# An encoder layer on one Trainium2 core: S5 tables on VectorE alone, q, k, v ahead in priority, and u, q, k, v, z as products of fp32r halves

## The chip, the cores and the metric

The kernel runs on one core of a Trainium2 chip. The metric is the device time of one execution in microseconds. Three runs of the kernel before gave 893.8, 893.03 and 889.67 us, median 893.03. Engines are named as the profile names them: PE is TensorE, DVE VectorE, ACT ScalarE, POOL GpSimd, SP SyncE.

## What is computed

One encoder layer on a sequence of 512 tokens of width 1024, in fp32. After an RMS norm, one weight of 1024 x 2576 is multiplied in and its columns are split; the change touches the projections of u, q, k, v and z (512 columns each) and of 16 gate columns, and the tables of the S5 scan that consumes u.

```python
h = _rmsnorm(x, norm_mix)
u, q, k, v, z, beta_f, beta_b, a_f, a_b = _split_cols(h @ w_in[l])
# u: S5, a diagonal complex recurrence in both directions, 32 groups of 16 channels, 64 states
lam_bar = jnp.exp(lam * step)
b_bar = ((lam_bar - 1.0) / lam)[:, :, None] * b
bu = jnp.einsum('gpc,bsgc->bsgp', b_bar, u.astype(jnp.complex64))
...
# q, k, v: 5-tap depthwise conv, silu, l2 norm of q and k, then gated delta rule in chunks of 64,
# with a triangular solve for each chunk, head and direction; z gates the result by silu(z)
```

After the two mixers come an output projection, cross attention to a memory of 256 tokens, and a mixture of 32 experts, two for each token.

## The kernel before

Everything is transposed: the normed input lies as `ht`, 128 partitions x 8 x 512, and one projection of 128 output columns (`proj`) loads a weight tile `wst` of 128 x 8 x 128 by SP's queue and multiplies 8 pieces of it with 8 pieces of `ht` into one PSUM bank (`mm8`, L143). There are 20 of them: 4 for u, 12 for q, k and v, 4 for z. The memory's k and v projections use `mm8` as well, with `mt` in place of `ht`, 256 columns wide.

The order of the work is set in two ways. The program merges generators (`weave`), and within the order of the program a scheduler that simulates the timeline places each engine's instructions; each engine then runs its queue in order, and waits where an operand or a buffer isn't there. The stages, with the profile's times:

- 0 to 66 us: the norm's transposes (L125), the u projections, the gates (L539), and the S5 parameters, small operations on DVE, ACT and POOL. `pw` holds powers of the diagonal.
- 66 to about 214 us: `weave((qkv, 13), (s5, 9))`. One stream is the 12 projections of q, k, v; each result goes through ACT (`xp`, `cv`), four conv products on DVE (L639, `cv`), a silu, PE transposes (L648) and, for q and k, a norm (L661 to L674). The other stream is the S5 groups, 8 of them: for each group two complex tables of 128 x 2 x 512 are made by `cmul` (L225 to L230): `pm`, which PE transposes (L372) and ACT copies to `bct`, and `ca`, which SP stores to `ca_scr`. PE then multiplies `uperm` with `bct` (L404, into `U`) and `bb` with `ca` (L381), and DVE copies that into `wl` (L387 to L390). `pm`, `ca` and `bct` have one buffer each. Two tables by hand say which engine makes each: of the 16, 9 are made on POOL (`CA_ENG` and `PM_ENG`, 1 is POOL), 7 on DVE.
- about 202 to 300 us: `weave((inv, 16), (rest(), 13), (rec, 17))`. `gdn_inv` forms the triangular matrices in four blocks (PE L703, L716, L717; DVE `e` L707, `N` L720), transposes them (`NT`, L731 and L734), solves by substitution on DVE (L742, L744), transposes the result (`XT`, `XN`, L749 and L750) and multiplies halves on PE (L768 and after). `rest` is the four z projections and 8 steps of the memory's k and v projections; `rec` (L414 to L417) is the S5 recurrence, 62 steps of four small DVE operations on `U`.
- about 300 to 435 us: `gdn_chain` beside the rest of the memory's projections and of `rec`, then the S5 output. 435 to 600 us: output projection and cross attention, whose products are already formed of fp32r halves by `mm3` (L149 to L151): each operand is split in a high part rounded to fp32r and a low part, the remainder, and low x high, high x high and high x low are added up. From 600 us: the experts.

Of the kernel before, what the change touches and what calls it, by code (L numbers as in the profile page):

```python
# [9 lines left out]
F32 = mybir.dt.float32  # L10
F32R = mybir.dt.float32r
# [20 lines left out]
P = 128  # L32
# [11 lines left out]
def weave(*streams):  # L44

    live = [[g, n, 0] for g, n in streams]
    while live:
        s = min(live, key=lambda t: (t[2] + 0.5) / t[1])
        s[2] += 1
        if next(s[0], s) is s:  # L50
            live.remove(s)


CA_ENG = (1, 1, 0, 1, 1, 1, 0, 1)
PM_ENG = (0, 0, 1, 0, 1, 0, 1, 0)


class Enc:
# [44 lines left out]
        return t  # L103


    def rms_T(self, pool, tiles, gain, out, tag, between=None, junk=None):

        nc = self.nc
        n = len(tiles)
        ss = pool.tile([P, 8], F32, name=tag + "ss", bufs=1)  # L110
        rs = pool.tile([P, 8], F32, name=tag + "rs", bufs=1)
        xn = []
        for i, t in enumerate(tiles):
            sq = junk if junk is not None else pool.tile([P, D], BF16, name=tag + "sq", bufs=1)
            nc.scalar.activation(sq, t, AF.Square, accum_out=ss[:, i:i + 1])
            nc.vector.tensor_scalar(ss[:, i:i + 1], ss[:, i:i + 1], 1.0 / D, 1e-6, op0=OP.mult, op1=OP.add)
            nc.gpsimd.tensor_tensor(rs[:, i:i + 1], ss[:, i:i + 1], self.nhalf[:, 0:1], op=OP.pow)
            nc.vector.tensor_scalar(t, t, rs[:, i:i + 1], None, op0=OP.mult)
            xn.append(t)
        if between:  # L120
            between()
        for k in range(8):
            ps = self.ps("tp")
            for i in range(n):
                nc.tensor.transpose(ps[:, i * P:(i + 1) * P],  # L125
                                    xn[i].rearrange("t (p k) -> t k p", k=8)[:, k, :], self.ident)
            src = ps[:, :n * P]
            if k % 2:
                nc.vector.tensor_scalar(out[:, k, :], src, gain[:, k:k + 1], None, op0=OP.mult)
            else:  # L130
                nc.scalar.activation(out[:, k, :], src, AF.Copy, scale=gain[:, k:k + 1])
        return xn

    def wcols(self, src, w):

        t = self.wp.tile([P, 8, w], F32, name="wst", bufs=4)
        self.nc.sync.dma_start(t, src)
        return t

    def mm8(self, ps, w, act):  # L140

# [12 lines left out]
    def stage_a(self):  # L154
        nc, tc, A = self.nc, self.tc, self.A
        pool = self.pa
        gain = self.col8('norm_mix', self.cp)
        x2d = A['x'][0]
        xt = []
        with tc.tile_pool(name="xp", bufs=1) as xp:  # L160
            for i in range(4):
                t = xp.tile([P, D], F32, name=f"x{i}")
                nc.sync.dma_start(t, x2d[i * P:(i + 1) * P, :])
                xt.append(t)
            self.ht = pool.tile([P, 8, T], F32, name="ht")
            self.pre = {}

            def first_weights():
                for c0 in (0, P):
                    self.pre[c0] = self.wcols(self.w_in(c0, P), P)  # L170
                self.w_g = self.wp.tile([P, 8, 16], F32, name="wg", bufs=1)
                nc.sync.dma_start(self.w_g, self.w_in(2560, 16))

            self.rms_T(xp, xt, gain, self.ht, "h", first_weights)

    def w_in(self, c0, w):
        return self.A['w_in'][0].rearrange("(p k) n -> p k n", k=8)[:, :, c0:c0 + w]

    def proj(self, c0):

        w = self.pre.pop(c0, None)
        if w is None:
            w = self.wcols(self.w_in(c0, P), P)
        ps = self.ps("mm")
        self.mm8(ps, w, self.ht)
        return ps

    def proj_u(self):
# [32 lines left out]
    def cmul(self, eng, pool, ore, oim, are, aim, bre, bim, shape, tag):  # L221
# [7 lines left out]
        eng.tensor_tensor(oim, aim, bre, op=OP.mult)  # L229
        eng.tensor_tensor(oim, oim, t2, op=OP.add)  # L230

    def s5_params(self):
        nc, A, tc = self.nc, self.A, self.tc
        sp = self.s5p
        v, g_ = nc.vector, nc.gpsimd
        with tc.tile_pool(name="s5t", bufs=1, side="right") as tq:
            ct = tq.tile([P, 2, 32, 16], F32, name="ct")
            dT = tq.tile([16, 32], F32, name="dT")
            aF = tq.tile([P, 2, 8, 32], F32, name="aF")
            aR = tq.tile([P, 2, 8, 32], F32, name="aR")  # L240
            bb = tq.tile([P, 2, 34, 16], F32, name="bb")
            b1 = tq.tile([P, 2, 32, 16], F32, name="b1")
            with tc.tile_pool(name="s5i", bufs=1, side="right") as tp:
                lamrow = tp.tile([32, 2, 128], F32, name="lamrow")
                for di, dn in enumerate('fb'):
# [26 lines left out]
                for ri in range(2):  # L272
                    ps = self.ps("s5")
                    for b in range(4):
                        nc.tensor.transpose(ps[:, b * P:(b + 1) * P], crow[:, ri, b, :], self.ident)
                    nc.scalar.activation(ct[:, ri].rearrange("p g c -> p (g c)"), ps, AF.Copy, scale=1.0 - 2.0 * ri)
# [66 lines left out]
                self.cmul(v, tp, b1[:, 0], b1[:, 1], bg(pw[:, 0, 1]), bg(pw[:, 1, 1]), bb[:, 0, :32], bb[:, 1, :32], [32, 16], "d")  # L343
            yield
            with tc.tile_pool(name="s5l", bufs=1, side="right") as tl:

# [5 lines left out]
                for gg in range(8):  # L352
# [3 lines left out]
                    bm = lambda b, ri: b[:, ri, gs, None, :].to_broadcast([P] + shp)  # L356

                    pm = tl.tile([P, 2] + shp, F32, name="pm", bufs=1)
                    e = PM_ENG[gg]
                    self.cmul((v, g_)[e], tl, pm[:, 0], pm[:, 1], am(aF, 0), am(aF, 1), bm(b1, 0), bm(b1, 1), shp, f"P{1 - e}")  # L360

                    ca = tl.tile([P, 2] + shp, F32, name="ca", bufs=1)
                    e = CA_ENG[gg]
                    self.cmul((v, g_)[e], tl, ca[:, 0], ca[:, 1], am(aR, 0), am(aR, 1),
                              bm(ct, 0), bm(ct, 1), shp, f"P{1 - e}")
                    nc.sync.dma_start(self.ca_scr[gg], ca.rearrange("p r g m c -> p (r g m c)"))

                    bcT = tl.tile([P, 4, 2, P], F32, name="bct", bufs=1)
# [148 lines left out]
    def gates(self):  # L517
# [6 lines left out]
        with tc.tile_pool(name="gt_", bufs=1) as tp:  # L524
# [9 lines left out]
            sel = tp.tile([P, 16], F32, name="gsel")  # L534
            v.tensor_reduce(sel, self.ident.rearrange("p (i c) -> p c i", i=4)[:, :16], axis=AX.X, op=OP.add)
            for j in range(2):
                for i in range(4):
                    k = j * 4 + i
                    nc.tensor.matmul(ps[i * 32:i * 32 + 16], self.w_g[:, k], self.ht[:, k], start=(j == 0), stop=(j == 1))  # L539
            for i in range(4):  # L540
                nc.scalar.activation(gT[i * 32:i * 32 + 16], ps[i * 32:i * 32 + 16], AF.Copy)
            pt = self.ps("tp")
# [133 lines left out]
    def proj_z(self):  # L676
        nc = self.nc
        for h in range(4):
            ps = self.proj(2048 + h * P)
            z = self.wp.tile([P, T], F32, name="zt", tag="ut", bufs=1)  # L680
            nc.scalar.activation(z, ps, AF.Silu)
            nc.sync.dma_start(self.z_scr[:, h], z)
            yield
# [823 lines left out]
    def build(self):  # L1507
# [41 lines left out]
        with tc.tile_pool(name="gi", bufs=2) as gi:  # L1549
            qkv = self.gdn_in([(w, n, h) for h in range(4) for w, n in ((1, "k"), (0, "q"))] +  # L1550
                              [(2, "v", h) for h in range(4)], gi)
            s5 = self.s5_params()
            next(s5)
            for _ in u:
                pass
            weave((qkv, 13), (s5, 9))

        self.gp2 = pool(left, "gp2")
        self.gp3 = pool(left, "gp3")
# [218 lines left out]
```

## Time and profile before

| what | value |
|---|---|
| median of 3 runs | 893.03 us |
| the profiled execution | 892.26 us |
| its span in the profile | 890.5 us |
| mean granted clock of PE | 0.948 |
| PE busy | 783.1 us (88%) |
| DVE, ACT, POOL busy | 404.3, 329.4, 232.6 us |
| projections from `ht` (L143) on PE | 151.3 us in 320 instructions |
| memory read, written | 165.50, 26.18 MB |

The profiled execution is 1.8 us longer than its span, and 0.8 us shorter than the median. A busy PE is not PE at its peak: matmuls are pipelined and the records of neighbours overlap, so the distance from start to start tells more than a record's length. PE's fp32 matmuls are two instructions each, which is why 160 matmuls of the projections are 320. Idle time is shown with what ended it, as the name of an engine and the tile that it wrote. Where a group's mean mixes cases (an operation that runs alone, or beside another engine), the timeline separates them.

### The profile page before, as it was taken

What the parts mean: (1) busy time and instruction counts of PE and PEld (TensorE: products, weight loads), DVE (VectorE), ACT (ScalarE), POOL (GpSimd) and SP (SyncE); (2) the same over time, 40 slices, a digit from 0 to 9 for tenths busy, and PEclk for the clock granted to TensorE, in tenths of its full rate; (3) what the DMA queues carried; (4) which work ended last, traced back from release to release, by engine and by line L of the source; (5) the groups of instructions that cost most, each with busy time, mean ns of one, the idle gap of its engine ahead of it and who ended that gap; (6) DMA issues with size and microseconds to landing.
All of it is one profiled execution on the core that took longest, in us unless ns stands there. A gap on an engine that the chain in (4) does not pass through costs nothing. (4 is left out here: it accounts for less than half of the span.)

```text
span 890.5 us, 12981 instructions
## 1 busy us (share of the span) xinstructions
PE 783.1 (88%) x4735; PEld 492.2 (55%) x4736; DVE 404.3 (45%) x1044; ACT 329.4 (37%) x760; POOL 232.6 (26%) x237
## 2 busy tenths in 40 slices
PE   5986998998997997899899999996698878788983
PEld 3443554555586875676688879895333333333331
DVE  4288767678899522244643554324210000000375
ACT  4242454455413235465343464333232131312204
POOL 1022857832100111205161332241311011100103
PEclk9996998999997998999999999998799999999997
DMA  7837222322663308615663714595699999999982
GB/s 206 144 91 111 74 78 74 100 76 98 225 193 104 108 24 169 116 56 172 184 224 96 260 49 159 194 406 187 248 391 412 414 411 408 395 391 410 410 350 102
DMA packets 128130, 185.17 MB, mean 208 GB/s; under 512 B 38734, under 2 KB 93006, under 8 KB 123968
## 3 DMA queue, kind: packets, MB, share of 16 engines
q1 hardware_dynamic: 122736, 172.31, 57.6%
q0 software_dynamic: 5328, 12.01, 3.6%
q8 instruction: 38, 0.62, 0.3%
q14 instruction: 28, 0.23, 0.1%
HBM read 165.50 MB, written 26.18 MB: 215 GB/s over the span
## 5 line engine op out<-in xcount | busy, mean ns | idle before, releaser
L143 PE MATMUL bank<-ht,wst 128*128 128x512 f32 x320 | 151.3, 621 | 4.2 <-ACT kd L583 2.4
L1340 PE MATMUL bank<-mw,xt 128*64 128x512 f32 x360 | 104.5, 595 | 1.5 <-DMA mw<-in_moe_w_up_dram 1.5
L143 PEld LDWEIGHTS bank<-ht,wst 128*128 128x128 f32 x320 | 60.7, 198 | 73.4 <-issue 68.3
L1344 DVE SCALAR_TENSOR_TENSOR hs<-hs,tw,bank 128x256 f32<-128x256 f32 x16 | 7.7, 480 | 168.9 <-ACT hs L1343 168.9
L1343 ACT ACTIVATE hs<-bank,tw 128x256 f32<-128x256 f32 x16 | 7.6, 474 | 155.5 <-PE bank L1340 155.5
L1380 PE MATMUL bank<-mw,hT 128*64 128x512 f32 x152 | 50.6, 660 | 16.2 <-ACT yd L1385 16.2
L1340 PEld LDWEIGHTS bank<-mw,xt 128*64 128x64 f32 x360 | 33.5, 138 | 55.6 <-issue 52.4
L143 PE MATMUL bank<-mt,wst 128*128 128x256 f32 x256 | 59.9, 393 | 0.0
L639 DVE SCALAR_TENSOR_TENSOR cv<-xp,taps,cv 128x512 f32<-128x512 f32 x48 | 50.4, 1049 | 20.8 <-ACT cv L637 19.7
L972 POOL TENSOR_TENSOR wlo<-wst,whi 128x1024 fp32r<-128x1024 f32 x16 | 38.6, 2416 | 78.7 <-ACT whi L971 78.7
L143 PEld LDWEIGHTS bank<-mt,wst 128*128 128x128 f32 x256 | 50.0, 198 | 7.7 <-issue 0.6
L1320 POOL DMA_INDIRECT xg<-t_scr,tidx x16 | 16.5, 1029 | 136.4 <-PE bank L1327 133.4
L824 POOL TENSOR_TENSOR kt<-kn,kd 64x512 f32<-64x512 f32 x14 | 14.5, 1035 | 97.6 <-PE bank L778 49.8
L1330 ACT ACTIVATE xt<-bank,gm 128x128 f32<-128x128 f32 x128 | 34.7, 382 | 8.9 <-PE bank L1327 7.8
L149 PE MATMUL bank<-wlo,oh 128*128 128x256 f32 x128 | 36.6, 289 | 0.0
L854 DVE SCALAR_TENSOR_TENSOR S<-S,egl,bank 128x128 f32<-128x128 f32 x48 | 15.5, 345 | 46.1 <-PE bank L851 46.1
L150 PE MATMUL bank<-whi,oh 128*128 128x256 f32 x128 | 35.8, 283 | 0.0
L1380 PEld LDWEIGHTS bank<-mw,hT 128*64 128x64 f32 x152 | 14.0, 148 | 38.7 <-issue 20.8
L151 PE MATMUL bank<-whi,ol 128*128 128x256 f32 x128 | 35.3, 287 | 0.0
L149 PE MATMUL bank<-mlo,mxh 128*128 128x512 f32 x64 | 25.8, 405 | 0.8 <-DVE gss L484 0.8
L903 POOL TENSOR_TENSOR mlo<-mst,mhi 128x512 fp32r<-128x512 f32 x16 | 22.0, 1393 | 14.8 <-ACT mhi L902 14.2
L150 PE MATMUL bank<-mhi,mxh 128*128 128x512 f32 x64 | 25.7, 402 | 0.0
(551 smaller groups left out, 1826.3 us busy)
## 6 DMA issues: line engine op xcount, KB each, us to landing
mw<-in_moe_w_down_dram SPq DMA_DIRECT2D x23, 1024.0 KB, 14.7
mw<-in_moe_w_gate_dram SPq DMA_DIRECT2D x45, 512.0 KB, 8.3
mw<-in_moe_w_up_dram SPq DMA_DIRECT2D x45, 512.0 KB, 13.9
wst<-in_w_in_dram SPq DMA_DIRECT2D x20, 512.0 KB, 4.5
ca_scr<-ca SPq DMA_DIRECT2D x8, 512.0 KB, 2.7
wst<-in_xa_wk_dram SPq DMA_DIRECT2D x8, 512.0 KB, 4.3
y_scr<-lhc SPq DMA_DIRECT2D x2, 2048.0 KB
wst<-in_xa_wv_dram SPq DMA_DIRECT2D x8, 512.0 KB, 4.3
```

What stands on the lines that cost most here:

```text
L143: self.nc.tensor.matmul(ps, w[:, k, :], act[:, k, :], start=(k == 0), stop=(k == 7))
L149: self.nc.tensor.matmul(ps, ah, bl, start=(first and i == 0), stop=False)
L150: self.nc.tensor.matmul(ps, ah, bh, start=False, stop=False)
L151: self.nc.tensor.matmul(ps, al, bh, start=False, stop=(last and i == n - 1))
L639: v.scalar_tensor_tensor(cv, xp[:, w:w + T], taps[:, w, m:m + 1], cv, op0=OP.mult, op1=OP.add)
L854: v.scalar_tensor_tensor(sn, S[di, h], self.egl[:, ch % 2, ch // 2, di * 4 + h:di * 4 + h + 1], p, op0=OP.mult, op1=OP.add)
L903: nc.gpsimd.tensor_tensor(lo[:, k], st, hi[:, k].bitcast(F32), op=OP.subtract)
L972: nc.gpsimd.tensor_tensor(lo, st, hi.bitcast(F32), op=OP.subtract)
L1320: self.gather = g_.indirect_dma_start(out=xg, out_offset=None, in_=self.t_scr, in_offset=bass.IndirectOffsetOnAxis(ap=self.tidx[:, q:q + 1 ...
L1330: nc.scalar.activation(xt[:, k], ps[:, (k % 4) * P:(k % 4 + 1) * P], AF.Copy, scale=self.gm[:, k:k + 1])
L1340: nc.tensor.matmul(pg[w * 64:w * 64 + 64].rearrange("p (a n) -> p a n", a=2), xt[:, k, w * 64:w * 64 + 64], un[k // 4 * 2 + w][:, :, k % 4 ...
L1380: nc.tensor.matmul(py[w * 64:w * 64 + 64], hT[:, k, w * 64:w * 64 + 64], wd[w][:, k, c], start=(k == 0), stop=(k == 1))
```

## The change

Three things are changed.

- The 16 S5 tables are all made on DVE, by `cprod`: four products of 128x512 and one addition of 128x1024, in place of four products and two additions of 128x512. For that `ct` and `b1` get a third, negated row, so that the subtraction becomes an addition; two copies on ACT fill these rows.
- The generator of q, k and v is stepped under `tc.high_priority()` (`ahead`), so that the scheduler prefers its instructions.
- `proj` uses `mm3`: `rms_T` writes the normed input as two fp32r tiles, `hth` (ACT) and `htl` (DVE, the remainder), and `wsplit` forms `whi` (ACT) and `wlo` (a subtraction) of every weight tile. `wlo` is formed on DVE for u2, u3 and all of q, k, v, and on POOL for u0, u1 and z. `wst` has 3 buffers in place of 4, `whi` and `wlo` two each. A projection is 24 matmuls. The gate columns are multiplied in fp32 with both halves, 16 matmuls in place of 8.

```diff
+def ahead(tc, g):
+    while True:
+        with tc.high_priority():
+            if next(g, g) is g:
+                return
+        yield
...
             src = ps[:, :n * P]
-            if k % 2:
+            if lo is not None:
+                nc.scalar.activation(out[:, k, :], src, AF.Copy, scale=gain[:, k:k + 1])
+                nc.vector.scalar_tensor_tensor(lo[:, k, :], src, gain[:, k:k + 1], out[:, k, :].bitcast(F32),
+                                               op0=OP.mult, op1=OP.subtract)
+            elif k % 2:
...
-        t = self.wp.tile([P, 8, w], F32, name="wst", bufs=4)
+        t = self.wp.tile([P, 8, w], F32, name="wst", bufs=3)
...
+    def wsplit(self, src, w, lo_eng):
+        st = self.wcols(src, w)
+        hi = self.wp.tile([P, 8, w], F32R, name="whi", bufs=2)
+        lo = self.wp.tile([P, 8, w], F32R, name="wlo", bufs=2)
+        self.nc.scalar.activation(hi, st, AF.Copy)
+        lo_eng.tensor_tensor(lo, st, hi.bitcast(F32), op=OP.subtract)
+        return hi, lo
...
-    def proj(self, c0):
-        w = self.pre.pop(c0, None)
-        if w is None:
-            w = self.wcols(self.w_in(c0, P), P)
+    def proj(self, c0, lo_eng=None):
+        hi, lo = self.pre.pop(c0, None) or self.wsplit(self.w_in(c0, P), P, lo_eng or self.nc.vector)
         ps = self.ps("mm")
-        self.mm8(ps, w, self.ht)
+        self.mm3(ps, [((hi[:, k, :], lo[:, k, :]), (self.hth[:, k, :], self.htl[:, k, :])) for k in range(8)])
         return ps
...
+    def cprod(self, pool, o, am, a, bm, b):
+        v = self.nc.vector
+        t = pool.tile(list(o.shape), F32, name="cpt", bufs=1)
+        for ri in range(2):
+            v.tensor_tensor(o[:, ri], am(a, 0), bm(b, 1 + ri), op=OP.mult)
+            v.tensor_tensor(t[:, ri], am(a, 1), bm(b, ri), op=OP.mult)
+        v.tensor_tensor(o, o, t, op=OP.add)
...
-                    e = PM_ENG[gg]
-                    self.cmul((v, g_)[e], tl, pm[:, 0], pm[:, 1], am(aF, 0), am(aF, 1), bm(b1, 0), bm(b1, 1), shp, f"P{1 - e}")
+                    self.cprod(tl, pm, am, aF, bm, b1)
...
-                    e = CA_ENG[gg]
-                    self.cmul((v, g_)[e], tl, ca[:, 0], ca[:, 1], am(aR, 0), am(aR, 1),
-                              bm(ct, 0), bm(ct, 1), shp, f"P{1 - e}")
+                    self.cprod(tl, ca, am, aR, bm, ct)
...
-                for i in range(4):
-                    k = j * 4 + i
-                    nc.tensor.matmul(ps[i * 32:i * 32 + 16], self.w_g[:, k], self.ht[:, k], start=(j == 0), stop=(j == 1))
+                for part in (self.htl, self.hth):
+                    for i in range(4):
+                        k = j * 4 + i
+                        nc.tensor.matmul(ps[i * 32:i * 32 + 16], self.w_g[:, k], part[:, k].bitcast(F32),
+                                         start=(j == 0 and part is self.htl), stop=(j == 1 and part is self.hth))
...
-            ps = self.proj(2048 + h * P)
+            ps = self.proj(2048 + h * P, nc.gpsimd)
...
-            weave((qkv, 13), (s5, 9))
+            weave((ahead(tc, qkv), 13), (s5, 9))
```

The change adds 29 lines ahead of the S5 stage, so a line there has a number higher by 27 to 29 in the kernel changed; the new products are L256 to L258, `wlo` is L157, and `mm3` L169 to L171.

The change also moves work. On DVE, at the first tables, the queue before reads as follows (`P` are the temporaries of `cmul`, `b_392` is `b1`, `cv` the conv products, `mt` the memory's norm, `dd` a small diagonal).

```order
L348 MEMSET dd 128x128
L225 TENSOR_TENSOR P_637<-aF,b_392 128x512
L226 TENSOR_TENSOR P_638<-aF,b_392 128x512
L593 COPY csr<-sbe 64x4x4 x2
L227 TENSOR_TENSOR pm<-aF,b_392 128x512
L229 TENSOR_TENSOR pm<-aF,b_392 128x512
L350 TENSOR_TENSOR dd<-ident,dT 16x128 x4
L228 TENSOR_TENSOR pm<-pm,P_637 128x512
L230 TENSOR_TENSOR pm<-pm,P_638 128x512
L225 TENSOR_TENSOR P_754<-aF,b_392 128x512
L226 TENSOR_TENSOR P_755<-aF,b_392 128x512
L639 SCALAR_TENSOR_TENSOR cv<-xp,taps,cv 128x512 x2
```

And the same place of DVE's queue in the kernel changed (`cpt` is the temporary of `cprod`).

```order
L157 TENSOR_TENSOR wlo<-wst,whi 128x1024
L668 SCALAR_TENSOR_TENSOR cv<-xp,taps,cv 128x512
L378 MEMSET dd 128x128
L256 TENSOR_TENSOR pm<-aF,b_449 128x512 x2
L257 TENSOR_TENSOR cpt<-aF,b_449 128x512
L256 TENSOR_TENSOR ca<-aR,ct 128x512 x2
L257 TENSOR_TENSOR cpt<-aF,b_449 128x512
L668 SCALAR_TENSOR_TENSOR cv<-xp,taps,cv 128x512
L380 TENSOR_TENSOR dd<-ident,dT 16x128 x4
L140 TENSOR_SCALAR mt<-bank_418,c_norm_mem 128x256
L157 TENSOR_TENSOR wlo<-wst,whi 128x1024
L258 TENSOR_TENSOR pm<-pm,cpt 128x1024
```

Now the table `ca` of the first group stands on DVE too, and the subtractions for `wlo` stand between the tables' operations.

On PE, at the start of the inverse, the queue before has a z projection (the L143 rows with `bank_1801` and `bank_1868`; `bank_1688` is a v projection) between one block and the next (a block is L703, then L716 and L717).

```order
L143 MATMUL bank_1688<-ht,wst 128x512 x4
L648 MATMUL bank_1708<-ident,cv 128x128 x4
L703 MATMUL bank_1750<-lef,g 64x64 x8
L703 MATMUL bank_1750<-geb,g 64x64 x8
...
L143 MATMUL bank_1801<-ht,wst 128x512 x8
L703 MATMUL bank_1817<-lef,g 64x64 x8
L703 MATMUL bank_1817<-geb,g 64x64 x7
L648 MATMUL bank_1719<-ident,cv 128x128 x4
...
L143 MATMUL bank_1868<-ht,wst 128x512 x8
L703 MATMUL bank_1884<-lef,g 64x64 x8
```

In the kernel changed the same place reads as follows; `bank_2199` and `bank_2286` are z1 and z2, L431 and L408 are the matmuls of the last S5 group, and L732, L745 and L746 those of the blocks.

```order
L171 MATMUL bank_2199<-hth,wlo 128x512
L169 MATMUL bank_2286<-htl,whi 128x512
L170 MATMUL bank_2286<-hth,whi 128x512
L431 MATMUL bank_1928<-uperm,bct 64x64 x2
...
L677 MATMUL bank_2026<-ident,cv 128x128 x4
...
L732 MATMUL bank_2057<-lef,g 64x64 x8
L732 MATMUL bank_2057<-geb,g 64x64 x8
L745 MATMUL bank_2165<-kT 64x64
L746 MATMUL bank_2165<-qT,kT 64x64
...
L732 MATMUL bank_2144<-lef,g 64x64 x8
```

z0, z1 and two matmuls of z2 have moved ahead of the last S5 group and so of the blocks, and blocks 0 and 1 now follow each other without a projection between them. Ten of the memory's projections, in place of nine, stand ahead of the matmuls on `XT` and `N` (L768 before, L797 now).

## Rows read from the trace of the kernel before

**Rows 1.** The page's slices, 40 of 22.3 us: PE's busy tenths.
```profile
PE   5986998998997997899899999996698878788983
```
**Rows 2.** The windows: us, then each engine's busy time, PE's clock, DMA share, GB/s.
```profile
66.00:202.00 136.00, 122.88 (x827) 65.59 (x826) 99.52 (x141) 60.12 (x168) 78.38 (x82) 0.92 0.35 85
202.00:281.00 79.00, 70.74 (x480) 49.60 (x479) 72.96 (x297) 25.14 (x36) 10.38 (x6) 0.97 0.54 174
281.00:435.00 154.00, 142.09 (x1186) 109.21 (x1183) 66.66 (x186) 73.02 (x155) 31.88 (x47) 0.93 0.44 110
600.00:890.00 290.00, 231.92 (x1141) 100.64 (x1139) 64.47 (x151) 74.75 (x218) 49.27 (x57) 0.93 0.89 349
```
**Rows 3.** Groups by line, 66 to 202 us, PE: busy, mean ns, idle before and releaser.
```profile
L143 PE MATMUL bank<-ht,wst 128*128 128x512 f32 x170 | 83.0, 635 | 0.0
L381 PE MATMUL bank<-ca,bb 64*32 64x128 f32 x256 | 13.7, 286 | 4.0 <-POOL xp L634 4.0
L404 PE MATMUL bank<-uperm,bct 128*64 128x64 f32 x256 | 11.3, 228 | 1.4 <-ACT bct L373 1.4
L372 PE MATMUL bank<-ident,pm 128*128 128x128 f32 x64 | 10.2, 292 | 7.6 <-DVE pm L228 7.4 <-POOL pm L230 0.2
```
**Rows 4.** The same groups, 66 to 202 us, DVE.
```profile
L639 DVE SCALAR_TENSOR_TENSOR cv<-xp,taps,cv 128x512 f32<-128x512 f32 x44 | 47.4, 1077 | 20.8 <-ACT cv L637 19.7
```
**Rows 5.** The timeline of DVE: start, us, instruction, idle before.
```profile
66.24 0.69 DVE L225 TENSOR_TENSOR P<-aF,b 128x512 f32<-128x512 f32 x1
66.85 0.68 DVE L226 TENSOR_TENSOR P<-aF,b 128x512 f32<-128x512 f32 x1
...
97.73 5.07 DVE L639 SCALAR_TENSOR_TENSOR cv<-xp,taps,cv 128x512 f32<-128x512 f32 x4 [4.22 <-ACT cv L637]
...
104.41 1.75 DVE L229 TENSOR_TENSOR ca<-aR,ct 128x512 f32<-128x512 f32 x1
...
113.93 3.11 DVE L639 SCALAR_TENSOR_TENSOR cv<-xp,taps,cv 128x512 f32<-128x512 f32 x4 [3.38 <-ACT cv L637]
```
**Rows 6.** The timeline of POOL at the same place.
```profile
102.22 1.72 POOL L228 TENSOR_TENSOR pm<-pm,P 128x512 f32<-128x512 f32 x1
```
**Rows 7.** The timeline of PE: gates, a projection, a block and the z behind it.
```profile
27.67 1.91 PE L539 MATMUL bank<-ht,wg 128*16 128x512 f32 x16
...
35.18 7.03 PE L143 MATMUL bank<-ht,wst 128*128 128x512 f32 x16
...
225.47 0.69 PE L703 MATMUL bank<-lef,g 128*64 128x64 f32 x16
...
227.53 7.13 PE L143 MATMUL bank<-ht,wst 128*128 128x512 f32 x16
```
**Rows 8.** The timeline of PE in the mix stage, products of halves.
```profile
457.47 0.40 PE L149 MATMUL bank<-mlo,mxh 128*128 128x512 f32 x1
457.70 0.39 PE L150 MATMUL bank<-mhi,mxh 128*128 128x512 f32 x1
```
**Rows 9.** Groups by line, whole span: splitting weights and halves, an add of 128x1024.
```profile
L972 POOL TENSOR_TENSOR wlo<-wst,whi 128x1024 fp32r<-128x1024 f32 x16 | 38.6, 2416 | 78.7 <-ACT whi L971 78.7
L971 ACT ACTIVATE whi<-wst 128x1024 fp32r<-128x1024 f32 x16 | 17.0, 1062 | 17.5 <-PE bank L151 10.7 <-DMA wst<-in_xa_wq_dram 4.6 <-issue 1.6
L1733 DVE TENSOR_TENSOR xr<-xr,yb 128x1024 f32<-128x1024 f32 x8 | 9.5, 1217 | 1.7 <-DMA yb<-y_scr 1.7
L1002 DVE TENSOR_TENSOR kvl<-kvs,kvh 128x1024 fp32r<-128x1024 f32 x4 | 6.2, 1562 | 10.0 <-ACT kvh L1001 10.0
```
**Rows 10.** Groups by line, 202 to 281 us, PE and DVE.
```profile
L143 PE MATMUL bank<-mt,wst 128*128 128x256 f32 x144 | 31.2, 379 | 0.0
...
L417 DVE TENSOR_TENSOR U<-U,rt 128x64 f32<-128x64 f32 x44 | 9.5, 216 | 0.5
L720 DVE SCALAR_TENSOR_TENSOR N<-bank,beta,e 128x64 f32<-128x64 f32 x32 | 6.7, 276 | 4.1 <-ACT e L710 4.1
```
**Rows 11.** The timeline of PE at the first matmuls behind the solve.
```profile
280.68 6.82 PE L768 MATMUL bank<-XT,N 32*32 32x32 f32 x128 [5.81 <-issue]
```

More of the change, by code (lines that the diff above doesn't have):

```diff
@@ L51, in weave @@
             live.remove(s)
-CA_ENG = (1, 1, 0, 1, 1, 1, 0, 1)
-PM_ENG = (0, 0, 1, 0, 1, 0, 1, 0)
+def ahead(tc, g):
[4 more added lines that the diff above has]
+        yield
 class Enc:
@@ L103, in colt, with rms_T @@
         return t
-    def rms_T(self, pool, tiles, gain, out, tag, between=None, junk=None):
+    def rms_T(self, pool, tiles, gain, out, tag, between=None, junk=None, lo=None):
         nc = self.nc
@@ L164, in stage_a @@
                 xt.append(t)
-            self.ht = pool.tile([P, 8, T], F32, name="ht")
+            self.hth = pool.tile([P, 8, T], F32R, name="hth")
+            self.htl = pool.tile([P, 8, T], F32R, name="htl")
             self.pre = {}
@@ L169, in first_weights @@
                 for c0 in (0, P):
-                    self.pre[c0] = self.wcols(self.w_in(c0, P), P)
+                    self.pre[c0] = self.wsplit(self.w_in(c0, P), P, nc.gpsimd)
                 self.w_g = self.wp.tile([P, 8, 16], F32, name="wg", bufs=1)
                 nc.sync.dma_start(self.w_g, self.w_in(2560, 16))
-            self.rms_T(xp, xt, gain, self.ht, "h", first_weights)
+            self.rms_T(xp, xt, gain, self.hth, "h", first_weights, lo=self.htl)
     def w_in(self, c0, w):
         return self.A['w_in'][0].rearrange("(p k) n -> p k n", k=8)[:, :, c0:c0 + w]
-    def proj(self, c0):
-        w = self.pre.pop(c0, None)
-        if w is None:
-            w = self.wcols(self.w_in(c0, P), P)
+    def proj(self, c0, lo_eng=None):
+        hi, lo = self.pre.pop(c0, None) or self.wsplit(self.w_in(c0, P), P, lo_eng or self.nc.vector)
         ps = self.ps("mm")
-        self.mm8(ps, w, self.ht)
+        self.mm3(ps, [((hi[:, k, :], lo[:, k, :]), (self.hth[:, k, :], self.htl[:, k, :])) for k in range(8)])
         return ps
@@ L236, in s5_params @@
         with tc.tile_pool(name="s5t", bufs=1, side="right") as tq:
-            ct = tq.tile([P, 2, 32, 16], F32, name="ct")
+            ct = tq.tile([P, 3, 32, 16], F32, name="ct")
             dT = tq.tile([16, 32], F32, name="dT")
@@ L241, in s5_params @@
             bb = tq.tile([P, 2, 34, 16], F32, name="bb")
-            b1 = tq.tile([P, 2, 32, 16], F32, name="b1")
+            b1 = tq.tile([P, 3, 32, 16], F32, name="b1")
             with tc.tile_pool(name="s5i", bufs=1, side="right") as tp:
@@ L275, in s5_params @@
                         nc.tensor.transpose(ps[:, b * P:(b + 1) * P], crow[:, ri, b, :], self.ident)
-                    nc.scalar.activation(ct[:, ri].rearrange("p g c -> p (g c)"), ps, AF.Copy, scale=1.0 - 2.0 * ri)
+                    nc.scalar.activation(ct[:, 1 + ri].rearrange("p g c -> p (g c)"), ps, AF.Copy, scale=1.0 - 2.0 * ri)
+                nc.scalar.activation(ct[:, 0].rearrange("p g c -> p (g c)"), ps, AF.Copy)
                 tl = lambda s: tp.tile([P, 32], F32, name="q" + s)
@@ L342, in s5_params @@
                 self.cmul(v, tp, bb[:, 0, :32], bb[:, 1, :32], bg(fre), bg(fim), bt[:, 0], bt[:, 1], [32, 16], "d")
-                self.cmul(v, tp, b1[:, 0], b1[:, 1], bg(pw[:, 0, 1]), bg(pw[:, 1, 1]), bb[:, 0, :32], bb[:, 1, :32], [32, 16], "d")
+                self.cmul(v, tp, b1[:, 1], b1[:, 2], bg(pw[:, 0, 1]), bg(pw[:, 1, 1]), bb[:, 0, :32], bb[:, 1, :32], [32, 16], "d")
+                nc.scalar.activation(b1[:, 0], b1[:, 2], AF.Copy, scale=-1.0)
             yield
```

## The prediction

> **What bounds the kernel now.** I read the page's slices first. PE is at 8 or 9 tenths over most of the span [rows 1], so the whole-kernel busy shares say little, and I went on by stage. The windows give three facts. From 66 to 202 us, the stretch in which q, k and v are projected beside the S5 tables, PE is busy 122.9 of 136 us while VectorE shows 99.5 and GpSimd 78.4 [rows 2]. From 202 to 281 us VectorE is the fuller engine, 73.0 of 79 us, with PE at 70.7 [rows 2]. From 600 us on DMA is at 0.89 [rows 2]: the expert weights bound that part, and their loads start when the stages ahead hand back SBUF, so whatever is gained ahead should move this tail as a whole.
>
> Next I asked what PE does in the first stretch. 83.0 us of its busy time are fp32 projections; the S5 matmuls and table transposes are 13.7, 11.3 and 10.2 us [rows 3]. The idle rows show that the tables can hold PE: 7.4 us are put down to VectorE's pm, and 4.0 us to GpSimd's xp, a small memset that stands behind table work on GpSimd [rows 3].
>
> Then I asked why VectorE is so busy. Its conv products cost 1.08 us each on average [rows 4]. Four of them in a row take 3.11 us from 113.93, while GpSimd is quiet, but 5.07 from 97.73 [rows 5], when GpSimd runs a pm table, 1.72 us for one of its subtractions [rows 6]. The tables' own 128x512 products start 0.61 us apart when GpSimd is quiet, and one takes 1.75 beside it [rows 5]. So two engines that both read large tiles slow one another. VectorE's idle time there is mostly for ScalarE's cv, 19.7 us in all [rows 4]: for the next projection to arrive.
>
> **The change, part by part.** All terms are against the profiled execution, 892.26 us (span 890.5); the median of the runs is 0.8 us above it.
>
> *Projections.* Before, a projection is 16 PE instructions and lasts 7.03 to 7.13 us [rows 7]. After it is 24 fp32r matmuls; in the mix stage such matmuls start 0.23 us apart [rows 8]: 24 x 0.23 = 5.5 us, so 1.5 us less, twenty times. The four u projections give back 6 us; against it stand the gate matmul, which doubles, +1.9 us [rows 7], the splitting of their own weights, two of them on GpSimd, and PE's wait for both halves of the norm's output. I count the u part as zero, between 4 us lost and 5 gained.
>
> *Splitting the weights.* Each wst now needs a rounded copy on ScalarE, 1.06 us, and a remainder [rows 9]. ScalarE has room. On VectorE no 128x1024 subtraction of this form exists; the plain add of that shape takes 1.22 and the nearest fp32r remainder 1.56 [rows 9]; I take 1.2, since it has the same two SBUF operands as the add. Nine such remainders lie among the tables (the others before the first table or on GpSimd), 10.8 us, at most 14. On GpSimd each takes 2.4 us [rows 9]; four are z's, late, when no table is left there.
>
> *Tables.* Sixteen tables, each four 128x512 products and one 128x1024 add: 4 x 0.61 + 1.22 = 3.7 us, 58 in all. Seven were on VectorE already and cost the same there alone (6 x 0.61); nine come over from GpSimd, +33 us. In return VectorE's slowed operations go back to their lone price: 44 conv products from 1.08 to 0.78 (a quarter of the 3.11), some 13 us, and its two ca tables up to 12 x (1.75 - 0.61) = 14.
>
> The sum for VectorE, from the first table to the first step of the recurrence: tables 58, conv 34, remainders 11, all else (wl, dd, vc, ss, mt) about 11: 114 us. For PE in the same stretch, 12.5 projections at 5.55 are 69, and its other work is the window's busy time less the projections, 122.9 - 83.0 = 40, taken as 46 since records of both overlap: 115 us. So the two are level. PE's idle time was 13 us there; I keep a little over half, 8, since GpSimd's part of it goes but single buffers (ca, pm) and two of whi and wlo stay. The first table starts at 66.2 now [rows 5]; two remainders, 2.4 us, come ahead of it, so 69. The recurrence then starts at 69 + 115 + 8 = 192 us, in place of 201.7.
>
> *Order around the inverse.* Before, z projections stand between the inverse's blocks, 7.13 us each [rows 7], and VectorE's block work waits on them. After, two z and the first matmuls of a third are ahead of block 0, and no conv product follows the first recurrence step. From that step to the XT,N matmuls, which now start at 280.7 [rows 11], 79 us pass. After, PE has 1.9 z (10.5 us), four blocks of 2.1 (225.47 to 227.53, [rows 7]) and ten kv projections in place of nine, 31.2 / 9 = 3.47 each [rows 10]: 54 us. VectorE had 73.0 us; by the order, 115 recurrence instructions stand ahead of XT in place of 176, each 0.22 us [rows 10], so 13 less, and conv, 3 less: 57, and 4 for ScalarE's e, as now [rows 10]: 61. VectorE sets it: XT,N at 192 + 61 = 253, that is 27.7 us earlier, plus 3.5 for the kv projection that no longer follows: 31 us. The 61 recurrence instructions that now come behind XT lie in VectorE's slack, busy 66.7 of 154 us there [rows 2].
>
> 892.3 - 31 = 861, and I forecast **861 us**. SP carries ca_scr stores and wst loads in one queue; a wst load that waits for VectorE's remainder holds back the ca store behind it, and so the next ca: 2.7 us eight times if never covered, covered here by the next pm (3.7 us).
>
> [...]
>
> **Rivals.**
> - *VectorE doesn't get faster.* If the slowed operations have another cause than GpSimd, VectorE's load is 99.5 + 33 + 11 = 143 us in the stretch, the recurrence starts at 69 + 143 = 212, XT,N at 273: 7.7 + 3.5 earlier, **881**. Against it: the same instruction has both durations, by whether GpSimd runs. 0.10.
> - *The engines trip over each other.* PE's projection needs ScalarE's rounding, which needs a free buffer from the projection two earlier, and VectorE's remainder in a queue of tables. With two full engines in order, the idle time of before (13 on PE) stays and 10 more come: the recurrence at 207, XT,N at 268, **876**. For it: the 7.4 us for pm [rows 3]. 0.16.
> - *Slower: the remainder becomes the wait.* If for each projection PE waits through one table (3.7) and the rounding (1.06) before the remainder is there, 12.5 x 4.7 = 58 us come on top of 115: the recurrence at 242, XT,N at 303, 22 later, with the kv projection's 3.5 back **911**. It decides against the change from about 2.5 us of wait per projection (31 us of gain over 12.5). For it: in-order VectorE, two buffers. Against it: PE has 46 us of other work to put between. 0.06; milder forms that end level, 0.08.
> - *Projections no faster.* If fp32r with alternating weights ran at the 0.40 us that a record lasts instead of the 0.23 us spacing [rows 8], 24 would last 9.4 us, +2.3 each, slower by some 25. The spacing in the mix stage has the same three-product pattern, so 0.02, within the slower chance.
>
> **How the numbers follow.** The main case, 0.58, has its own range from 847 (no stall left and a first table at 64) to 874 (lone prices high: remainder 1.56, stalls 20). With the first two rivals the time is under 888.5 in 0.84. What a measurement can tell from no change is about 0.5%, 4.5 us. Level 0.08, slower 0.08. The range of 8 in 10 runs from 844 to 885.
>
> **What would show it.** Right: four conv products in 3.1 us throughout; GpSimd near empty from 70 to 170 us; 24 matmuls in 5.5 us; the first recurrence step near 192 and XT,N near 253. Wrong: PE idle after 70 us put down to wlo or ca; remainders of 2 us; an unchanged 79 us from recurrence to XT,N; a clock below 0.9 where PE now waits; or a shift at XT,N that the tail from 600 us does not show.

## The result, and the profile after

The changed kernel takes 878.41 us, median of four executions (872.87 to 885.89), against 891.75 for the kernel before beside them (889.67 to 893.8): a ratio of 0.9856, interval 0.9815 to 0.9896. It is faster by 1.4%, less than half as much as forecast: 861 us would have been a ratio of 0.965. The profiled execution took 872.87 us, with a span of 871.1 and a mean granted clock of 0.932, where before it was 890.5 and 0.948. It is the fastest of the four; the slowest, 885.89 us, ran at a mean clock of 0.915, so the readings below account for 19.4 us of gain, and the median keeps 13.3 of them. Of the ten executions each of the kernels tables and mt_w8 below, the two slowest, over 1.5% above their fastest and at a lower clock, are left out of medians, ranges and ratios.

The windows of the changed kernel, two of them cut as those of before [rows 2], and then by its own stages (us, busy time of PE, PEld, DVE, ACT, POOL, PE's clock, DMA share, GB/s):

```profile
66.00:202.00 136.00, 125.08 (x1220) 100.01 (x1219) 129.96 (x239) 81.25 (x194) 34.29 (x36) 0.99 0.49 133
281.00:435.00 154.00, 143.04 (x883) 106.02 (x883) 58.98 (x149) 66.04 (x130) 30.54 (x48) 0.84 0.46 120
66.00:187.00 121.00, 110.62 (x964) 87.68 (x964) 116.77 (x186) 73.97 (x184) 28.43 (x33) 1.00 0.47 115
187.00:245.10 58.10, 56.04 (x471) 48.02 (x466) 55.45 (x234) 16.69 (x28) 9.48 (x6) 0.98 0.57 190
245.10:414.70 169.60, 157.55 (x1183) 120.03 (x1183) 80.15 (x253) 74.76 (x155) 32.29 (x49) 0.83 0.40 103
```

Up to the first matmuls on XT and N the forecast is kept and exceeded: the recurrence starts at 187.0 and XT,N at 245.1, as the instructions of these two lines and the timeline show.

```profile
L441 DVE TENSOR_TENSOR rt<-a8r,U x62: 206/224/1076, 187.0 to 286.5; 128x64 f32<-128x64 f32 x62
```
```profile
245.13 5.27 PE L797 MATMUL bank<-XT,N 32*32 32x32 f32 x128 [1.03 <-issue]
```

That answers to 280.68 before [rows 11]: 35.6 us earlier. At the first matmul of the mix stage only 20.9 of them are left (414.7 against 435.6), and at the end 19.4. So the gain was made where it was looked for, and two fifths of it were given back between XT,N and the mix, in code that the diff does not touch. The last window above says how: PE's clock is 0.83 there. Before, the same stretch went

```profile
280.70:435.60 154.90, 142.41 (x1189) 109.56 (x1189) 67.39 (x188) 73.32 (x155) 31.96 (x48) 0.93 0.44 109
```

I call "lost to the clock" the sum, over thirty equal windows of a stretch, of a window's length times one minus its granted clock. It is 11.5 us before and 29.0 after; what is left of the stretch is 143.4 and 140.6. The sum counts windows in which PE itself waits too, so it is the most that the clock can have cost. The account of the profiled execution: -35.6 to XT,N, -2.8 for the rest of that stretch (one kv projection fewer), +17.5 lost to the clock, +1.5 behind: -19.4.

### The profile page after: what moved, and what is told of

Same layout as the page of the kernel before. It is cut to its first block, busy times and chain, and to the rows that moved or that the text cites. A ratio compares the mean times of both kernels' runs of the same rounds, so it can differ in the third digit from the quotient of the medians.

```text
span 871.1 us, 13365 instructions
## 1 busy us (share of the span) xinstructions
PE 771.9 (89%) x4911; PEld 533.1 (61%) x4912; DVE 422.1 (48%) x1100; ACT 348.3 (40%) x783; POOL 180.3 (21%) x189
## 5 line engine op out<-in xcount | busy, mean ns | idle before, releaser
L1369 PE MATMUL bank<-mw,xt 128*64 128x512 f32 x360 | 106.4, 604 | 1.9 <-DMA mw<-in_moe_w_up_dram 1.9
L169 PE MATMUL bank<-htl,whi 128*128 128x512 f32 x160 | 66.1, 414 | 4.4 <-ACT cv L666 2.0
L171 PE MATMUL bank<-hth,wlo 128*128 128x512 f32 x160 | 64.1, 402 | 0.0
L170 PE MATMUL bank<-hth,whi 128*128 128x512 f32 x160 | 64.0, 400 | 0.0
L1409 PE MATMUL bank<-mw,hT 128*64 128x512 f32 x152 | 48.8, 646 | 16.2 <-ACT yd L1414 16.2
L668 DVE SCALAR_TENSOR_TENSOR cv<-xp,taps,cv 128x512 f32<-128x512 f32 x48 | 39.3, 829 | 0.1
L169 PEld LDWEIGHTS bank<-htl,whi 128*128 128x128 f32 x160 | 31.0, 194 | 13.4 <-ACT cv L666 2.9
L883 DVE SCALAR_TENSOR_TENSOR S<-S,egl,bank 128x128 f32<-128x128 f32 x48 | 15.8, 346 | 46.8 <-PE bank L880 46.8
L169 PE MATMUL bank<-wlo,oh 128*128 128x256 f32 x128 | 36.6, 289 | 0.0
L1409 PEld LDWEIGHTS bank<-mw,hT 128*64 128x64 f32 x152 | 13.6, 146 | 37.6 <-issue 19.6
L171 PE MATMUL bank<-whi,ol 128*128 128x256 f32 x128 | 35.3, 287 | 0.0
L171 PEld LDWEIGHTS bank<-hth,wlo 128*128 128x128 f32 x160 | 30.7, 192 | 6.6
## 6 DMA issues: line engine op xcount, KB each, us to landing
mw<-in_moe_w_down_dram SPq DMA_DIRECT2D x23, 1024.0 KB, 13.2
```

Of the source, the lines that this page charges most:

```text
L169: self.nc.tensor.matmul(ps, ah, bl, start=(first and i == 0), stop=False)
L170: self.nc.tensor.matmul(ps, ah, bh, start=False, stop=False)
L171: self.nc.tensor.matmul(ps, al, bh, start=False, stop=(last and i == n - 1))
L668: v.scalar_tensor_tensor(cv, xp[:, w:w + T], taps[:, w, m:m + 1], cv, op0=OP.mult, op1=OP.add)
L883: v.scalar_tensor_tensor(sn, S[di, h], self.egl[:, ch % 2, ch // 2, di * 4 + h:di * 4 + h + 1], p, op0=OP.mult, op1=OP.add)
L1369: nc.tensor.matmul(pg[w * 64:w * 64 + 64].rearrange("p (a n) -> p a n", a=2), xt[:, k, w * 64:w * 64 + 64], un[k // 4 * 2 + w][:, :, k % 4 ...
```

## The experiments

Two theories stood first: C, that the clock differs from execution to execution, and O, that the order of the work behind XT,N is worse. Neither came out as written, and a third, G, was formed from their runs: that the order of the work around the GLU's products on PE sets its clock (the GLU is the gated product at the end of the S5 output, weights `wglu`).

**again: the same kernel.** No edit.

> The changed kernel once more. Theory C (the clock): ahead of the XT,N matmuls the gain is 33 to 37 us in every execution, and what is lost behind them is PE time at a granted clock of 0.50 between 300 and 420 us; so the start of XT,N comes within 2 us of 245, the stretch from XT,N to the end differs between executions by 5 us or more, and the executions with the lower mean clock are the longer ones. Theory O (the order): the work between XT,N and the mix is placed worse by the scheduler; then the stretch from XT,N to the first mix matmul is 169 to 171 us again, with the same instructions late.

872.5 us (871.45 to 873.51), clocks 0.930 to 0.934. XT,N at 244.7, the mix at 413.8: 169.1 us again, 28.9 of them lost to the clock. The low stretches fall at the same instructions: 0.50 from 380 to 388 and from 408 to 416 in both profiles. So the loss belongs to the kernel, not to an execution: C is right in its price, and O is right that the stretch repeats. C's scatter, longer executions at a lower clock, is not in these four; in the first four it was (872.9 us at 0.932 to 885.9 at 0.915).

**mm3: products of halves alone.**

```diff
-            self.ht = pool.tile([P, 8, T], F32, name="ht")
+            self.hth = pool.tile([P, 8, T], F32R, name="hth")
+            self.htl = pool.tile([P, 8, T], F32R, name="htl")
...
-        self.mm8(ps, w, self.ht)
+        self.mm3(ps, [((hi[:, k, :], lo[:, k, :]), (self.hth[:, k, :], self.htl[:, k, :])) for k in range(8)])
```

> The kernel before with the products of fp32r halves alone: tables as before on VectorE and GpSimd, no priority. By the prediction's terms PE has 1.5 us less for each projection, 18 us in the stretch of q, k and v, but VectorE gets nine remainders and keeps its slowed operations: the first recurrence step 5 to 10 us earlier than the 201.7 of before if PE was the bound, no earlier if VectorE is; time 880 to 892. Theory C: the granted clock decides a further 5 us either way. Theory O: the same gain at the end as at XT,N.

879.75 us, ratio 0.988 (0.982 to 0.994). The recurrence starts at 192.8, 8.9 us earlier, as expected if PE was the bound, and XT,N at 266.6, 14.1 us earlier; 12.0 lost to the clock behind it. The profiled span is 13.6 us shorter, so here the gain at XT,N did reach the end.

**tables: all tables on VectorE, nothing else.**

```diff
-                    self.cmul((v, g_)[e], tl, pm[:, 0], pm[:, 1], am(aF, 0), am(aF, 1), bm(b1, 0), bm(b1, 1), shp, f"P{1 - e}")
+                    self.cprod(tl, pm, am, aF, bm, b1)
...
-                    self.cmul((v, g_)[e], tl, ca[:, 0], ca[:, 1], am(aR, 0), am(aR, 1),
+                    self.cprod(tl, ca, am, aR, bm, ct)
```

> The kernel before with all sixteen tables on VectorE and nothing else: fp32 projections as before. VectorE's load goes from 99.5 to about 105 us in the stretch (33 more, some 27 back), PE keeps 122.9: no gain beyond PE's stalls, so the first recurrence step between 196 and 204, time 885 to 897. If GpSimd's traffic was what slowed VectorE, four conv products take 3.1 us and none takes over 1 us; if not, some still take 1.2 or more.

891.5 us (885.05 to 897.82, eight executions; all ten have the median 894.09), ratio 1.002 (0.997 to 1.007): by the time, nothing. By the trace, a great deal: the recurrence starts at 189.9, ahead of the 196 to 204 expected, and XT,N comes at 259.1, 21.6 us earlier; then the mix stage begins 171.4 us later, 27.6 of them lost to the clock. That the time lies in the expected range is luck: the loss behind XT,N took back a gain that was not expected. This is the changed kernel's loss without its priority and without its products of halves. The window from XT,N to the mix:

```profile
259.10:430.50 171.40, 160.81 (x1201) 122.28 (x1201) 73.19 (x222) 75.48 (x157) 32.29 (x49) 0.84 0.39 100
```

**mm3_tables: the changed kernel without the priority.**

```diff
-            weave((ahead(tc, qkv), 13), (s5, 9))
+            weave((qkv, 13), (s5, 9))
```

> The changed kernel without the priority for q, k and v. If the priority is worth something, the first recurrence step is 3 us or more later than 187; if not, it is within 2 us and the time is that of the changed kernel within the spread that theory C gives it, 872 to 886.

856.13 us (853.1 to 858.18), ratio 0.962 (0.956 to 0.969). The recurrence starts at 186.7, within 2 us, and XT,N at 247.1, 2 us later than with the priority; yet the kernel is 16 us faster than again on the same chip. The mix begins at 396.8, and the window from XT,N to it is

```profile
247.10:396.80 149.70, 139.28 (x1171) 106.25 (x1171) 81.23 (x246) 73.52 (x154) 32.36 (x48) 0.92 0.44 112
```

with 11.9 us lost to the clock. The expectation took an equal start of the recurrence to mean an equal time, and that failed.

What tells the kernels that lose 28 us from those that lose 12 is not in the edits but in the queue of PE. In before, mm3 and mm3_tables the GLU's sixteen wide products (`gt,wglu`, 512 columns) stand apart among the chain's narrow ones (128 columns at most); in after and tables the first eight stand in a clump. Counts of PE's instructions in the order of their queue, from the first product of the GLU on (`qkd` are the chain's outputs, `ot` transposes, `ones` matmuls of one column; most instructions of the queue are two in the trace):

```
spread (before, mm3, mm3_tables): wglu 1, chain 6, qkd 1, wglu 2, ot 4, wglu 3, qkd 1, ...
clump (after, tables):            wglu 3, chain 1, wglu 5, chain 2, ot 4, chain 4, qkd 1, ones 4, qkd 14, ...
```

The scheduler, which simulates the whole program, switches between the two when something far ahead is moved. The next four kernels move such things on purpose.

**first12: the priority on the first 12 steps, not on the last.** Its queue has the spread form.

```diff
+    i = 0
     while True:
-        with tc.high_priority():
+        i += 1
+        with (tc.high_priority() if i <= 12 else ExitStack()):
```

> The changed kernel with the priority on the first 12 steps of q, k, v and not on the last one. In its order the GLU's wide products stand spread among the chain's narrow ones, as in the kernel before, and not in a clump of eight as in the changed kernel. Theory G (the GLU's order sets PE's clock): XT,N stays at 244 to 248 us, but the time lost to the low clock between XT,N and the mix falls from 29 to about 12 us, and the time is 853 to 860. Theory P (the priority itself costs it): the clock is lost as in the changed kernel, time 870 to 880.

853.23 us (850.12 to 856.3), ratio 0.957 (0.950 to 0.965). XT,N at 245.0, as in the changed kernel; 151.2 us to the mix, 13.7 lost to the clock. Theory P is out: nearly all of the priority is still there.

**tables_w12: the tables alone, in the spread form.**

```diff
-            weave((qkv, 13), (s5, 9))
+            weave((qkv, 12), (s5, 9))
```

> The tables alone on VectorE with the weave of q, k, v and S5 at 12 to 9 in place of 13 to 9, which puts the GLU's wide products in the spread order of before. Theory G: XT,N within 3 us of the 259 that the tables alone gave, the loss to the clock behind it about 12 in place of 28 us, time 875 to 882. Otherwise (the loss belongs to the tables): 888 to 900 as with the tables alone.

868.52 us (867.54 to 869.66), ratio 0.975 (0.967 to 0.982): 23 us faster than tables, and below the 875 to 882 expected. The loss to the clock behind XT,N is 12.1, as theory G has it. XT,N at 255.9 is 3.2 us earlier than in tables, so the new weave brings something ahead of XT,N as well.

**mt_w8: mm3_tables, in the clump form.**

```diff
-            weave((qkv, 13), (s5, 9))
+            weave((qkv, 13), (s5, 8))
```

> Tables and products of halves, no priority, with the weave at 13 to 8, which puts the GLU's wide products into the clump of the changed kernel. Theory G: XT,N within 4 us of 247, the loss to the clock back at 27 to 30 us, time 870 to 880 though no priority is left. Theory P: 853 to 860.

878.3 us (871.3 to 883.07, eight executions; all ten have the median 879.47), ratio 0.985 (0.981 to 0.990). XT,N at 245.4, even earlier than in mm3_tables, and 29.8 lost to the clock: 22 us slower than mm3_tables, without any priority. Theory G holds in both directions.

**first06: the priority on six steps.** As first12, with 6 in place of 12; in its queue the chain is nearly complete before the GLU's products.

> The priority on the first 6 steps alone; its order has a third form, the chain complete but for one block's outputs before the GLU's products, which then stand in a clump at the end. Theory G gives no exact number for it: the narrow matmuls lie without wide ones between them, so a loss to the clock nearer 28 than 12 us, time 868 to 880; if the clump alone is what hurts, and not the narrow stretch, 855 to 862.

872.71 us, inside the expected range, but not for the expected reason: XT,N comes at 249.2, only 13.2 us are lost to the clock and the mix begins 154.4 us later. Against first12 some 4 us are lost up to XT,N, 3 up to the mix and 8 behind the mix's start, 5 of them while the mix's products run (first to last start 51.9 us against 46.8); I have not followed these further. So neither a chain without wide products between nor a clump at the end costs more of the clock here; what the three kernels with the great loss share is a clump ahead of the chain's last steps.

**lo_pool: remainders of q, k, v on GpSimd, no priority.**

```diff
-        hi, lo = self.pre.pop(c0, None) or self.wsplit(self.w_in(c0, P), P, lo_eng or self.nc.vector)
+        hi, lo = self.pre.pop(c0, None) or self.wsplit(self.w_in(c0, P), P, lo_eng or self.nc.gpsimd)
```

> Tables and products of halves without priority, with the remainders of q, k, v formed on GpSimd in place of VectorE (2.4 us each in place of 1.2); the GLU's order is the spread one. Theory V (VectorE bounds the stretch of q, k, v and the remainders are 11 us of its load): the first recurrence step comes 3 to 8 us earlier than the 186.7 of the same kernel with VectorE's remainders, time 848 to 854. Theory S (the shared traffic): GpSimd's remainders slow VectorE's conv products and tables by as much or more, conv mean above 0.9 us, first step at 186 or later, time 855 or more.

868.63 us, ratio 0.977 (0.971 to 0.982), 12 us over mm3_tables, each against before on its own chip. The first step comes at 184.8 against 186.7, 1.9 us earlier: less than theory V's 3 to 8, and ahead of theory S's 186. XT,N comes only at 259.7. GpSimd's remainder takes 2.86 us, not 2.4, and VectorE's operations pay (the conv product and the product into `pm` take 0.83 and 0.68 us on average in after):

```profile
L668 DVE SCALAR_TENSOR_TENSOR cv<-xp,taps,cv 128x512 f32<-128x512 f32 x45 | 43.8, 977 | 0.2
L256 DVE TENSOR_TENSOR pm<-aF,b 128x512 f32<-128x512 f32 x14 | 13.3, 993 | 0.0
...
L157 POOL TENSOR_TENSOR wlo<-wst,whi 128x1024 fp32r<-128x1024 f32 x12 | 34.3, 2862 | 14.7 <-ACT whi L156 9.7 <-PE bank L399 4.9
```

From 66 us to XT,N VectorE is busy 187.6 us, against 173.8 in mm3_tables: theory S is right in its cost and in the time.

**lo_half: every second remainder on GpSimd, in first12.**

```diff
+        ... lo_eng or (self.nc.vector, self.nc.gpsimd)[c0 // P % 2]
```

> The kernel of first12 with every second remainder of q, k, v on GpSimd. Theory V: first recurrence step 2 to 4 us earlier than 186.1, time 848 to 852. Theory S: no gain, 853 to 860. The GLU's order is the spread one, so the loss to the clock between XT,N and the mix is 11 to 14 us.

864.29 us (863.38 to 865.28), ratio 0.970 (0.965 to 0.975), first step at 183.3, XT,N at 250.2, 13.7 lost to the clock. Slower than first12b beside it by 9 us. The first step came as theory V has it, 2.8 us earlier, and no gain came of it; but the time is above theory S's 853 to 860 too. Of the 13.2 us between the two profiled executions 5.1 stand at XT,N, and the rest behind it, not followed.

**first12b: first12 again.**

> The kernel of first12 once more, unchanged, for its interval: 850 to 857, XT,N at 245, about 14 us lost to the clock up to the mix.

855.18 us (852.1 to 857.55, six executions), ratio 0.961 (0.957 to 0.964): the version that beats both kernels, 35 us under the kernel before.

The kernels side by side (XT,N and the mix's start from each trace; the stretch between them, what of it is lost to the clock, and the rest):

| kernel | GLU | us | XT,N | to the mix | lost | rest |
|---|---|---|---|---|---|---|
| before | spread | 889 | 280.7 | 154.9 | 11.5 | 143.4 |
| mm3 | spread | 879.8 | 266.6 | 152.7 | 12.0 | 140.7 |
| tables_w12 | spread | 868.5 | 255.9 | 154.7 | 12.1 | 142.6 |
| mm3_tables | spread | 856.1 | 247.1 | 149.7 | 11.9 | 137.8 |
| first12 | spread | 853.2 | 245.0 | 151.2 | 13.7 | 137.5 |
| tables | clump | 891.5 | 259.1 | 171.4 | 27.6 | 143.8 |
| after | clump | 878.4 | 245.1 | 169.6 | 29.0 | 140.6 |
| mt_w8 | clump | 878.3 | 245.4 | 170.6 | 29.8 | 140.8 |

The rest is 137.5 to 143.8 us in all of them. Pair by pair (tables and tables_w12, after and first12, mt_w8 and mm3_tables) the stretch is 16.7, 18.4 and 20.9 us longer in the clump form, and 15.5, 15.3 and 17.9 of these are lost to the clock, which in after falls from 1.00 to 0.50 in the windows below. Most of it lies at the end: from the GLU's first product to the mix the spread kernels take 35.3 to 36.8 us and lose 0.0 to 1.7, the clumped ones take 49.1 to 50.4 and lose 11.7 to 12.7. The windows of the GLU in after and in first12 show where:

```profile
372.00:376.00 4.00, 4.00 (x24) 2.20 (x22) 1.62 (x4) 3.02 (x6) 2.54 (x2) 1.00 0.42 152
376.00:380.00 4.00, 4.00 (x25) 3.99 (x25) 0.85 (x3) 2.39 (x4) 1.98 (x2) 0.64 0.76 212
380.00:384.00 4.00, 4.00 (x23) 3.41 (x21) 0.68 (x1) 0.65 (x2) 0.55 (x1) 0.50 0.54 187
...
408.00:412.00 4.00, 1.12 (x6) 0.72 (x5) 2.36 (x6) 0.63 (x1) 2.18 (x3) 0.50 0.99 349
```
```profile
366.00:370.00 4.00, 4.00 (x24) 2.16 (x23) 1.04 (x2) 3.08 (x6) 1.76 (x2) 1.00 0.80 221
370.00:374.00 4.00, 4.00 (x39) 3.71 (x38) 2.23 (x2) 2.03 (x6) 2.03 (x2) 1.00 0.56 187
374.00:378.00 4.00, 4.00 (x37) 3.46 (x35) 2.32 (x5) 1.38 (x3) 1.78 (x2) 1.00 0.47 135
```

And the timeline of PE there, in after and then in first12:

```profile
368.32 4.56 PE L502 MATMUL bank<-gt,wglu 128*128 128x512 f32 x10
...
378.12 0.63 PE L831 MATMUL bank<-vn,qkd 64*64 64x128 f32 x2
378.55 0.63 PE L832 MATMUL bank<-vn,qkd 64*64 64x128 f32 x2
```
```profile
371.10 0.38 PE L833 MATMUL bank<-vn,qkd 64*64 64x128 f32 x2
371.32 0.38 PE L834 MATMUL bank<-vn,qkd 64*64 64x128 f32 x2
```

In after the first eight wide products are done by 372.9. What follows are the chain's last dependent steps, transposes and four matmuls of one column each; the packed narrow outputs begin at 376.7, and from 377 the clock is low, until the next wide products run at 388 to 391. In first12 the packed outputs begin at 369.3, less than 2 us behind the wide products, the next wide ones follow at 378.8, and the clock stays at 1.00 up to 390. PE is "busy" 4.00 of 4.00 us in both, since the records of neighbours overlap (the L831 row of after at 378.12 lasts 0.63 us, and the L832 row starts 0.43 behind it). The count of instructions does not foretell the fall either: ahead of it there are 24 in 4 us at a clock of 1.00, and so there are in first12 from 366 to 370. Behind it the count is low by the clock itself, as the same pairs of outputs start 0.43 us apart at 0.50 and 0.22 at 1.00. Why the clock falls just there stays open; that the order of the work decides it is shown by the edits in both directions. They move all of the work behind XT,N, and the GLU's products with it; no run moves these alone. The windows above show the clock of after at 1.00 up to 376 and at 0.50 from 380 to 384, and the timeline of PE shows no idle time in between.

## Why the prediction was right and wrong

**Projections: right.** In the changed kernel the products of halves start 0.23 us apart, as taken from the mix stage [rows 8]:

```profile
104.36 0.40 PE L170 MATMUL bank<-hth,whi 128*128 128x512 f32 x1
104.59 0.39 PE L171 MATMUL bank<-hth,wlo 128*128 128x512 f32 x1
```

**VectorE's terms: right in the sum, and close one by one.** The groups of 66 to 187 us (busy, mean ns, idle before):

```profile
L668 DVE SCALAR_TENSOR_TENSOR cv<-xp,taps,cv 128x512 f32<-128x512 f32 x47 | 38.6, 831 | 0.1
L157 DVE TENSOR_TENSOR wlo<-wst,whi 128x1024 fp32r<-128x1024 f32 x10 | 12.2, 1217 | 0.5 <-ACT whi L156 0.5
L258 DVE TENSOR_TENSOR pm<-pm,cpt 128x1024 f32<-128x1024 f32 x8 | 10.8, 1356 | 0.0
```

The remainder is 1.22 us, as taken from the add [rows 9]; the conv product fell from 1.08 [rows 4] to 0.83 us, not quite to 0.78; GpSimd still forms z's four remainders there, 2.70 us each. In tables_w12, where GpSimd forms neither tables nor remainders, it is 0.75:

```profile
L647 DVE SCALAR_TENSOR_TENSOR cv<-xp,taps,cv 128x512 f32<-128x512 f32 x48 | 35.8, 747 | 2.1 <-ACT cv L645 1.0 <-POOL rs L674 0.3
```

The addition into `pm` is 1.36 us, not 1.22. From the first table, at 67.0 in place of 69, to the recurrence VectorE was forecast at 114 us and is busy 115.7 of 120.0; PE was forecast at 115 and is busy 110.6 of the 121 from 66 us. So VectorE, not PE, is the fuller engine, by a little, and the recurrence starts at 187.0 in place of 192. The stop at VectorE's pm [rows 3] is gone from PE's idle time. PE still idles 10.4 us, 13.1 before, now mostly for ScalarE's cv and bct, and the low clock is gone: 0.92 before [rows 2], 1.00 from 66 to 187 now. I had not counted that; by the sum defined above it is worth 10 us at most (10.3 lost to the clock before, 0.5 now). That the low clock hung on PE's waits is not shown: mm3_tables idles 14.4 us there and loses 1.7.

**The tables alone: I was wrong on what they are worth.** The prediction has no price for them alone, and the expectation for tables put them at no gain beyond PE's stalls, since PE bounded the stretch. With fp32 projections and the weave of before, tables starts its recurrence 11.8 us earlier and its XT,N 21.6; with the weave at 12 to 9, in tables_w12, it is 17.1 (184.6) and 24.8. PE is busy 121.7 of 123.9 us in the one and 116.9 of 118.6 in the other. PE had been the bound, but 13 of the 136 us were PE's waits and 10 more were lost to its clock; of the waits 2 are left, of the loss nothing. At the same weave the products of halves bring the rest of the 33.6 us by which XT,N is earlier in mm3_tables: 3.2 ahead of the recurrence's start (189.9 and 186.7), where VectorE, now with the remainders, is busy 116.3 of 120.7 us, and 8.8 behind it (69.2 us from there to XT,N in tables, 60.4 in mm3_tables, where two z projections stand ahead of the first block).

**Order around the inverse: right in size.** 61 us were forecast from the recurrence to XT,N; it is 58.1, with ten kv projections ahead of it. That VectorE sets it is not shown: PE is busy 56.0 of these 58.1 us and VectorE 55.5.

**What failed is the step "whatever is gained ahead should move this tail as a whole".** It is in the reading of the bound, and the sum took it over by carrying 31 us from XT,N to the end: the stretch from XT,N to the mix was put at its old length, less one kv projection, without a reason. The tail itself did as predicted, 454.9 us from the mix to the end before and 456.4 after. The stretch ahead of it became 14.7 us longer although the diff has no line there (17.5 more lost to the clock, 2.8 gained), because the scheduler put the work around the GLU's products in another order, which after's queue already showed and which I did not compare beyond the solve. Without that step the sum holds to 6 to 8 us: first12, which has the whole change but for one step's priority, takes 853 and 855 us in its two measurements, inside the main case's own range, and its XT,N at 245.0 is 8 us ahead of the 253 forecast.

**The rivals.** "VectorE doesn't get faster" is out by the conv product. "The engines trip over each other" named 876, close to what was measured, and by the wrong mechanism: no stall of 23 us is in the stretch, so that nearness is luck. "The remainder becomes the wait" is out: none of PE's idle time from 66 to 187 us is put down to whi or wlo. "Projections no faster" is out by the 0.23 us. Of the signs that I listed, a shift at XT,N that the tail does not show came: 35.6 us at XT,N, 19.4 at the end. A clock below 0.9 came too, but from XT,N to the mix, not in the stretch where PE waited before.

**The case against the change** was to leave the nine tables on GpSimd, with VectorE as full as it was [rows 2]. mm3 is that case beside mm3_tables, and takes 24 us more; lo_pool, with the remainders on GpSimd, takes 12 more. The conv product takes 0.75 us in tables_w12, where GpSimd forms neither tables nor remainders, and 0.98 in lo_pool, a mean over products that met a remainder and others that did not.

## What to carry to other kernels

Where a scheduler orders the whole program, compare the queue of the bounding engine up to the end, not only around the edit: a change far ahead can reorder a stage that it never names, and here that cost 16 to 23 us. Read PE's clock by stage before and after any change, since a busy share of 1 can stand beside a clock of 0.50, as in after from 380 to 384 us. Where work on one engine slows another, as GpSimd's remainders did the conv product here (0.75 us on average in tables_w12 without them, 0.98 in lo_pool with them), judge the move of work between the two by the lone durations, not by the shares of busy time.

## What was not expected of the hardware

In after PE's clock fell from 1.00 to 0.50 between 376 and 380 us while the profile showed no idle time of PE, and kernels that compute the same lose between 0.0 and 12.7 us to it from the GLU's first product to the mix.

The kernels also differ in scatter. The spread kernels with the tables on VectorE or products of halves stay within 8 us over four to six executions (mm3_tables 853.1 to 858.2, first12b 852.1 to 857.6); the kernel before varies by 11 to 13 us over eleven or thirteen, the changed kernel by 13 over its first four, tables and mt_w8 by 13 and 12 over eight. Why again kept to 2 us stays open, and no tie of the scatter to the order is shown.
